# Average pooling on one Trainium2 core: the first tile loaded by four transfers of strided partitions

## The chip, the cores and the metric

The kernel runs on one core of a Trainium2 chip. The metric is the time of one execution on the device, in microseconds; the kernel before took 333.46 us, the median of three runs from 333.3 to 333.56. A core has engines that compute (here VectorE, called DVE in the profile, ScalarE or ACT, and GpSimd or POOL), a sequencer for issuing transfers (SyncE or SP), 16 DMA engines that move data between the device memory (HBM) and the on-chip memory (SBUF), and SBUF itself, which has 128 partitions. TensorE (PE) has no work in this kernel.

## The reference

The input `x` is 32 x 256 x 4096 in float32 and `output_size` is 256. Each output value is the mean of a window along the last axis:

```python
for i in range(output_size):
    start = int(i * length / output_size)
    end = int((i + 1) * length / output_size)
    result[:, :, i] = np.mean(x[:, :, start:end], axis=-1)
```

Since 4096 is 16 times 256, every window has 16 neighbouring values. The input is 134.22 MB and the output 8.39 MB, so the work is nearly all reading.

## The kernel before

Batch and channel are flattened into 8192 rows of 4096 values. A tile holds four of these rows in each of the 128 partitions, which is 64 KB per partition and 8 MB in all, and there are 16 tiles. For the first 15 tiles a partition owns 60 consecutive rows of HBM (`x_many`), and tile `t` takes the columns `t * cols` to `(t + 1) * cols` of them; the last tile has its own block of rows (`x_last`). So for each partition a tile is one contiguous run of 64 KB in HBM and one contiguous run in SBUF.

The tiles pass through a pool of two buffers (`inpool`, L53). The loop from L62 does for each tile:

- L70: SP issues one transfer of the whole tile, 128 partitions, into the buffer `xin`. All 16 loads go through SP's queue, in order.
- L72, in the last tile only: SP issues the store of the results of the first 15 tiles (`o_many`, 60 KB per partition).
- L73: POOL adds, for the upper half of the windows, the second eight values of each window to the first eight.
- L78: DVE sums the 16 values of each window of the lower half.
- L81: DVE sums the eight values that POOL left of each window of the upper half.
- L84: ACT multiplies the tile's 1024 results by 1/16.

After the loop two stores bring out the last tile's results, 4 KB per partition: partitions 0 to 119, then 120 to 127 (L89 and L90, which calls `store`, L57). At the very end SP waits until all three stores have landed (L95).

The order of work around L70 is set by the tile framework, which derives the waits from the program: a compute instruction that reads `xin` waits for the landing of what was loaded into it, and a load into a buffer waits until the instructions that read its former contents are done and until its former load has landed. With two buffers the loads of tiles 0 and 1 are issued at once, and the load of tile 2 waits for the compute of tile 0. On each DMA engine packets run in the order in which they were queued. A packet of a load is one partition's 64 KB.

Of the kernel before, what the change touches and what calls it, by code (L numbers as in the profile page):

```python
# [1 line left out]

# [4 lines left out]


@with_exitstack
def kernel(  # L10
    ctx: ExitStack,
    tc: tile.TileContext,
    x: bass.AP,
    output_size: int,
    out: bass.AP,
):

    nc = tc.nc
    F32 = mybir.dt.float32
    X = mybir.AxisListType.X

    batch, channels, length = x.shape
    ob, oc, olen = out.shape
    assert ob == batch and oc == channels and olen == output_size
    assert length % output_size == 0
    window = length // output_size  # L30
    hw = window // 2
    inv_w = 1.0 / float(window)

    P = nc.NUM_PARTITIONS
    R = 4
    rows = batch * channels
    assert rows % (P * R) == 0
    ntiles = rows // (P * R)
    many = (ntiles - 1) * R
    cells = R * output_size  # L40
    m = cells // 2
    cols = R * length

    xr = x.rearrange("b c l -> (b c) l")
    orow = out.rearrange("b c o -> (b c) o")
    x_many = xr[0 : P * many, :].rearrange("(p r) l -> p (r l)", p=P, r=many)
    o_many = orow[0 : P * many, :].rearrange("(p r) o -> p (r o)", p=P, r=many)
    x_last = xr[P * many :, :].rearrange("(p r) l -> p (r l)", p=P, r=R)
    o_last = orow[P * many :, :].rearrange("(p r) o -> p (r o)", p=P, r=R)

    res_many = nc.alloc_sbuf_tensor("res_many", [P, (ntiles - 1) * cells], F32, align_bytes=256)
    res_last = nc.alloc_sbuf_tensor("res_last", [P, cells], F32, align_bytes=256)
    inpool = ctx.enter_context(tc.tile_pool(name="inpool", bufs=2))  # L53

    stored = nc.alloc_semaphore("stored")

    def store(out, in_):  # L57
        ins = nc.sync.dma_start(out=out, in_=in_)
        tc.no_tile_sem_insts.add(ins.ins.name)
        ins.then_inc(stored, 16)  # L60

    for t in range(ntiles):  # L62
        last = t == ntiles - 1
        xin = inpool.tile([P, cells, window], F32, name="xin")
        if last:
            res, base, src = res_last, 0, x_last
        else:
            res, base = res_many, t * cells
            src = x_many[:, t * cols : (t + 1) * cols]
        nc.sync.dma_start(out=xin.rearrange("p o w -> p (o w)"), in_=src)  # L70
        if last:
            store(o_many, res_many[:, :])  # L72
        nc.gpsimd.tensor_add(  # L73
            out=xin[:, m:cells, 0:hw],
            in0=xin[:, m:cells, 0:hw],
            in1=xin[:, m:cells, hw:window],
        )
        nc.vector.reduce_sum(  # L78
            out=res[:, base : base + m], in_=xin[:, 0:m, :], axis=X
        )  # L80
        nc.vector.reduce_sum(  # L81
            out=res[:, base + m : base + cells], in_=xin[:, m:cells, 0:hw], axis=X
        )
        nc.scalar.mul(  # L84
            out=res[:, base : base + cells],
            in_=res[:, base : base + cells],
            mul=inv_w,
        )
    for lo, hi in ((0, 120), (120, P)):  # L89
        store(o_last[lo:hi, :], res_last[lo:hi, :])  # L90

    ctx.pop_all().close()
    tc.close()
    tc.compile()  # L94
    nc.sync.wait_ge(stored, 48)  # L95
    nc.sync.sem_clear(stored)


# [1 line left out]
_INS = ['x', 'output_size']  # L100
_OUTS = [((32, 256, 256), 'float32')]

_NUMBERS = {'output_size': 256}


# [26 lines left out]
```

## Time and profile before

| What | Value |
|---|---|
| Median of three runs | 333.46 us |
| The profiled execution's own time | 333.37 us |
| Its span | 332.1 us |
| DVE busy | 209.7 us, 32 instructions |
| POOL busy | 139.7 us, 20 instructions |
| ACT busy | 18.2 us, 17 instructions |
| DMA packets | 2599, 142.61 MB, 99.4% of 16 engines' span |
| First packets of tile 0 / tile 0 landed | 1.8 us / 22.7 us |
| One POOL add (L73) | 8.719 us |
| One DVE sum of 16 (L78) / of 8 (L81) | 8.686 us / 4.420 us |

The span runs from the first to the last instruction of the profile; the execution's own time is a little longer. Engine shares are busy time over the span. The DMA share is the time that packets took, over 16 engines, and a window's share counts each packet at its start, so in short windows it can lie over 100%. A line number such as L70 is a line of the kernel before. "SPq" is SP's sequencer, which issues transfers.

### The profile page before, as it was taken

The page shows a single profiled execution, that of the slowest core. Times are in us where ns is not written, and L with a number is a line of the kernel's source. Part 1 is how long each engine was busy: PE and PEld are TensorE (multiplying, and loading weights), DVE is VectorE, ACT ScalarE, POOL GpSimd, SP SyncE. Part 2 cuts the span into 40 slices and gives each one's busy share as a digit, 9 for nine tenths or more (in the row PEclk, how much of TensorE's full clock was granted, in tenths as well). Part 3 has the DMA queues.
Part 4 walks back from the last instruction along what each step waited for, and adds up shares of the span by engine and source line. Part 5 has one row for each costly group of instructions (what it writes and reads, how often), then busy time and mean ns, then how long its engine had stood idle before and what let it go on. Part 6 is the DMA issues. An engine that isn't in the chain of part 4 may idle for free.

```text
span 332.1 us, 160 instructions
## 1 busy us (share of the span) xinstructions
DVE 209.7 (63%) x32; ACT 18.2 (5%) x17; POOL 139.7 (42%) x20
## 2 busy tenths in 40 slices
DVE  0029396692939669293966939295693929569392
ACT  1000101001010100101010010101000010100001
POOL 0027091542709164270916427090643709063270
DMA  9898999989899998989899998989999898989997
GB/s 379 379 505 379 474 411 426 458 379 505 379 489 395 450 434 379 505 379 505 379 474 411 395 489 379 505 379 489 395 450 434 379 505 379 505 379 474 395 466 307
DMA packets 2599, 142.61 MB, mean 429 GB/s; under 512 B 295, under 2 KB 295, under 8 KB 423
## 3 DMA queue, kind: packets, MB, share of 16 engines
q1 hardware_dynamic: 2599, 142.61, 99.4%
HBM read 134.22 MB, written 8.39 MB: 429 GB/s over the span
## 4 chain that ended last, share of the span: by engine, by line
DMA 66%; POOL 18%; DVE 11%; POOLq 3%; issue 0%; ACT 0%; SPq 0%
DMA xin<-in_x_dram 66%; POOL xin L73 18%; DVE res_many L81 9%; POOLq L94 3%; DVE res_last L81 1%; ACT res_last L84 0%; SPq L70 0%; POOLq L73 0%
## 5 line engine op out<-in xcount | busy, mean ns | idle before, releaser
L73 POOL TENSOR_TENSOR xin<-xin 128x4096 f32<-128x4096 f32 x16 | 139.5, 8719 | 181.7 <-DMA xin<-in_x_dram 181.7
L78 DVE TENSOR_REDUCE res_many<-xin 128x512 f32<-128x8192 f32 x15 | 130.3, 8686 | 107.4 <-DMA xin<-in_x_dram 107.4
L81 DVE TENSOR_REDUCE res_many<-xin 128x512 f32<-128x4096 f32 x15 | 66.3, 4420 | 2.5 <-POOL xin L73 2.3
L84 ACT ACTIVATE res_many<-res_many 128x1024 f32<-128x1024 f32 x15 | 15.9, 1057 | 289.8 <-DVE res_many L81 289.8
L78 DVE TENSOR_REDUCE res_last<-xin 128x512 f32<-128x8192 f32 x1 | 8.7, 8686 | 6.3 <-DMA xin<-in_x_dram 6.3
L81 DVE TENSOR_REDUCE res_last<-xin 128x512 f32<-128x4096 f32 x1 | 4.4, 4420 | 0.2 <-POOL xin L73 0.2
L84 ACT ACTIVATE res_last<-res_last 128x1024 f32<-128x1024 f32 x1 | 1.1, 1057 | 18.5 <-DVE res_last L81 18.5
L84 ACT ACT_TABLE_LOAD x1 | 1.3, 1283 | 0.7 <-PEq L113 0.7
L113 POOL MEMSET const-float32-0.0<- 128x1 f32 x1 | 0.1, 99 | 0.2 <-issue 0.2
L113 POOL MEMSET const-bfloat16-1.0<- 128x1 bf16 x1 | 0.1, 103 | 0.0
L113 POOL MEMSET const-uint8-127<- 128x1 uint8 x1 | 0.1, 103 | 0.0
L113 POOL MEMSET const-float32-1.0<- 128x1 f32 x1 | 0.1, 99 | 0.0
## 6 DMA issues: line engine op xcount, KB each, us to landing
out_dram<-res_many SPq DMA_DIRECT2D x1, 7680.0 KB
out_dram<-res_last SPq DMA_DIRECT2D x1, 480.0 KB
xin<-in_x_dram SPq DMA_DIRECT2D x16, 25.3
out_dram<-res_last SPq DMA_DIRECT2D x1, 32.0 KB
```

Source lines behind the costliest of these rows:

```text
L73: nc.gpsimd.tensor_add(out=xin[:, m:cells, 0:hw], in0=xin[:, m:cells, 0:hw], in1=xin[:, m:cells, hw:window],)
L78: nc.vector.reduce_sum(out=res[:, base : base + m], in_=xin[:, 0:m, :], axis=X)
L81: nc.vector.reduce_sum(out=res[:, base + m : base + cells], in_=xin[:, m:cells, 0:hw], axis=X)
L84: nc.scalar.mul(out=res[:, base : base + cells], in_=res[:, base : base + cells], mul=inv_w,)
L94: tc.compile()
L113: nc = _bacc.Bacc("TRN2", target_bir_lowering=False, num_devices=1)
```

## The change

The load of tile 0 is cut into four transfers by partitions: 0, 8, .., 120 (16 partitions), then 4, 12, .., 124 (16), then 2, 6, .., 126 (32), then the odd ones (64). Together they cover the 128 partitions once. SP issues them one after the other in place of the single one. For every other tile the list `parts` holds the one entry (0, 1), which is all the partitions in one transfer as before. What is computed, the buffers, the stores and the rest of the order of the program stay as they are.

```diff
@@ -67,7 +67,10 @@
         else:
             res, base = res_many, t * cells
             src = x_many[:, t * cols : (t + 1) * cols]
-        nc.sync.dma_start(out=xin.rearrange("p o w -> p (o w)"), in_=src)
+        flat = xin.rearrange("p o w -> p (o w)")
+        parts = ((0, 8), (4, 8), (2, 4), (1, 2)) if t == 0 else ((0, 1),)
+        for lo, step in parts:
+            nc.sync.dma_start(out=flat[lo:P:step, :], in_=src[lo:P:step, :])
         if last:
             store(o_many, res_many[:, :])
         nc.gpsimd.tensor_add(
```

## The prediction

> **What bounds the kernel now.** I read the page first: engine shares, DMA rows, the chain that ended last.
>
> ```profile
> DVE 209.7 (63%) x32; ACT 18.2 (5%) x17; POOL 139.7 (42%) x20
> ...
> DMA packets 2599, 142.61 MB, mean 429 GB/s; under 512 B 295, under 2 KB 295, under 8 KB 423
> ...
> q1 hardware_dynamic: 2599, 142.61, 99.4%
> ...
> DMA xin<-in_x_dram 66%; POOL xin L73 18%; DVE res_many L81 9%; POOLq L94 3%; DVE res_last L81 1%; ACT res_last L84 0%; SPq L70 0%; POOLq L73 0%
> ```
>
> The 16 DMA engines are busy 99.4% of the span and no compute engine over 63%, so the end is set by the longest of 16 rows of packets laid end to end. The POOL and DVE shares of the chain are only where the chain jumps from one transfer to the compute that frees its buffer: work beside the packets, as the timeline of tiles 0 and 1 shows next.
>
> ```profile
> 22.72 8.69 DVE L78 TENSOR_REDUCE res_many<-xin 128x512 f32<-128x8192 f32 x1 [22.72 <-DMA xin<-in_x_dram]
> 22.76 8.72 POOL L73 TENSOR_TENSOR xin<-xin 128x4096 f32<-128x4096 f32 x1 [22.32 <-DMA xin<-in_x_dram]
> 31.51 4.42 DVE L81 TENSOR_REDUCE res_many<-xin 128x512 f32<-128x4096 f32 x1
> 35.96 19.61 SPq L70 DMA_DIRECT2D xin<-in_x_dram  x2
> ...
> 42.00 8.69 DVE L78 TENSOR_REDUCE res_many<-xin 128x512 f32<-128x8192 f32 x1 [6.07 <-DMA xin<-in_x_dram]
> ```
>
> Tile 0 lands at 22.7 us, its buffer is free and tile 2 asked for at 35.96, and tile 1 is still streaming until 42.0: 6.0 us of cover. So whatever delays tile 0's packets delays the end one for one, and whatever delays only waits or issues by less than 6 us does not.
>
> Last I asked the DMA view for single waves of packets. The share is of 16 engines over the window, so share x window is the mean packet where the window holds the starts of 16 packets. Windows, in order: 1.7 to 4.7 us, 4.7 to 7.1, 309 to 311.5, and 330.6 to 331.2.
>
> ```profile
> DMA packets 16, 1.05 MB, mean 350 GB/s; under 512 B 0, under 2 KB 0, under 8 KB 0
> ...
> q1 hardware_dynamic: 16, 1.05, 104.3%
> ```
> ```profile
> DMA packets 16, 1.05 MB, mean 437 GB/s; under 512 B 0, under 2 KB 0, under 8 KB 0
> ...
> q1 hardware_dynamic: 16, 1.05, 100.8%
> ```
> ```profile
> DMA packets 16, 1.05 MB, mean 419 GB/s; under 512 B 0, under 2 KB 0, under 8 KB 0
> ...
> q1 hardware_dynamic: 16, 1.05, 107.6%
> ```
> ```profile
> DMA packets 58, 0.24 MB, mean 396 GB/s; under 512 B 0, under 2 KB 0, under 8 KB 58
> ...
> q1 hardware_dynamic: 58, 0.24, 96.1%
> ```
>
> A load packet is one 64 KB row of a partition. In the first wave it takes 1.043 x 3.0 = 3.13 us, in the second 1.008 x 2.4 = 2.42 us (27.1 GB/s), which is the rate of the whole run: tiles land 19.3 us apart, eight packets of 2.42. The third window is the last wave of the last tile, when the large store has been issued and its reads of SBUF begin: 1.076 x 2.5 = 2.69 us. The fourth is the final store's 4 KB rows: 0.961 x 0.6 x 16 / 58 = 0.159 us each (25.8 GB/s).
>
> **The change, part by part.** The sum is made against the profiled execution, 333.37 us (span 332.1 and 1.27 around it), 0.09 under the median 333.46 of the runs.
>
> *Issues on SP.* Tile 0 takes four issues instead of one. An issue costs 0.41 us plus 0.06 of gap (0.74 to 1.21), so they go out at 0.74, 1.21, 1.68 and 2.15, and tile 1's at 2.62 instead of 1.21. From issue to first packet took 1.04 us (0.74 to 1.78, where the DMA view's first packets start). The second transfer's rows are therefore queued at 2.25, the third's at 2.72, the fourth's at 3.19, tile 1's at 3.66, while the engines need them at 4.8, 7.2, 12 and 22 at the earliest. Cost 0, hidden by the packets in flight; uncovered, each would cost 0.47.
>
> *Start.* The first transfer now has one row per engine. Its issue may shorten from 0.41 us towards the 0.29 of the 8-row store, and the two late starters (14 of 16 first packets start between 1.78 and 2.1, one near 2.25, one near 2.79) may come with the others. Bounds: no gain, and all of the first wave's excess, 3.13 - 2.42 = 0.71. Nearest row is the issue: I take -0.1.
>
> *Completions.* Each transfer ends with a 4-byte entry on every engine it uses. The final 2.1 us hold 39 of them, 16 + 15 + 8, which shows 16, 15 and 8 engines at work on 128, 120 and 8 rows; so 16, 16, 32 and 64 rows give every engine 1, 1, 2 and 4, eight in all as before. Three more entries at 9 ns (that window's 20.70 us of packets less 128 x 0.159, over 39) are +0.03.
>
> *Waits.* The first POOL and DVE instructions wait for four landings instead of one, and SP's wait before tile 2 (17 ns, at 22.7) becomes four; what is queued behind it, tile 2's issue, waits for DVE L81 until 35.96 anyway. Hidden by 13.2 us there and by the 6.0 us of tile 1's packets; 0. Beyond 6.0 us a delay would leave the engines empty.
>
> *Two engines at neighbouring rows.* This decides. A transfer of 128 rows takes every group of four neighbouring partitions, and so do those at strides 4 and 2. The two at stride 8 take every second group, with all 16 engines at once. The trace of before has no strided load, so bounds: nothing, if an engine's 2.42 us is its own limit; and twice the time, if it is the limit of one of 16 paths into SBUF, each serving its own groups of neighbouring partitions: half the groups then hold half the paths, and two engines use one. Two packets per engine would take 4.84 us instead of 2.42, together +4.84. Rows towards nothing: the 4 KB rows of the final store, where 15 engines read 120 rows, eight each, and then eight engines read eight neighbouring rows, at 0.159 us throughout. Towards a cost: the 2.69 us wave, the one place where a load's writes meet a second stream on the SBUF side, at +0.27 a packet (two packets: +0.54); and that load rows from HBM and the large store's 60 KB rows to HBM (1.030 x 2.2 = 2.27 us in the window from 314 to 316.2) run at the same 27.1 GB/s, so that the ceiling is not HBM's direction. The changed operation is a write of 64 KB rows, nearer to the load rows, which sit exactly on that ceiling in every wave, than to short reads. I take the full price, less what a pair wins by not starting together (starts differ by 0.1 to 0.3 us): +4.6. A gain is excluded, since the 2.42 us wave is already the fastest in the trace.
>
> [...]
>
> [...]
>
> Sum: 333.37 + 0 - 0.1 + 0.03 + 0 + 4.6 = 337.9.
>
> **The rivals.**
> *No sharing, no change.* The engines' rate is their own and tile 0's rows only come in another order. Then 333.37 - 0.1 + 0.03 = 333.3, between 332.8 and 334.0. The store's rows speak for it, the load's constant rate against it.
>
> *Faster.* The one-row transfer removes most of the first wave's excess and its late start, on the engines that end last. It decides from 0.67 us (0.2%) on; the ceiling is 0.71 mean, so 332.7. Against: 3.13 us is seen on nearly all engines, the late one included, and an engine with one row queued still has to wait for its first bytes.
>
> *A wait between the four transfers.* If each is issued only when the one before has landed, an engine runs dry at three joins, at about 1.04 from issue to packet and 0.71 of a first packet: 3 x 1.75 = 5.3, 338.6. If the queues only restart, 3 x 0.71 = 2.1, 335.5. Against: the four write different partitions, and tiles 0 and 1 went out 0.47 apart without a gap.
>
> **How the numbers follow.** A repeat run differs by 0.1 us; 0.2%, 0.67 us, is about what a measurement tells from no change. Sharing 0.50 (own range 337.2 to 338.6; a milder sharing down to 334.5 is another 0.05); wait or restart 0.05; no change 0.31; faster 0.09. Slower holds 0.50 + 0.05 + 0.05 = 0.60, within 0.2% 0.31, faster 0.09. The two large cases lie on both ends, so the range must span 333 to 338.6: I give 332.9 to 338.7, which leaves out most of the faster case and the worst waits, about 0.12.
>
> **What would show it.** Right: tile 0 lands at about 27.3 us instead of 22.7, with two waves of packets near 4.8 us each before 12 us and waves of 2.42 after; every later landing shifted by the same 4.6; 2647 packets, 343 of them under 512 B; 19 load issues. Wrong: first two waves at 3.1 and 2.4 (no sharing); slices of idle DMA in the first 10 us (a wait); a landing before 22.2 (faster). It would also be wrong if the late start moved to an engine that carries nine rows of the final store, which I hold under 0.3 us.

## The result and the profile after

The changed kernel takes 338.36 us, the median of four runs (338.02 to 338.40), against 333.51 us (333.30 to 333.69) for the kernel before: a ratio of 1.0144, with a 95% interval from 1.0132 to 1.0156. The profiled execution took 338.35 us with a span of 337.0, 4.98 more than that of before (333.37, span 332.1). Line numbers of the changed kernel are three higher from the load on: L73 is the load, L76 POOL's add, L81 and L84 DVE's sums.

The page of the changed kernel shows the same compute and the same bytes, with 48 more packets, all of them 4-byte completion entries (three more transfers on 16 engines):

```profile
DVE 209.7 (62%) x32; ACT 18.2 (5%) x17; POOL 139.7 (41%) x20
...
GB/s 249 249 498 373 498 373 498 373 498 373 498 373 498 373 490 381 490 381 474 397 459 412 420 451 420 451 412 459 389 482 381 490 381 490 373 498 373 482 467 296
DMA packets 2647, 142.61 MB, mean 423 GB/s; under 512 B 343, under 2 KB 343, under 8 KB 471
...
q1 hardware_dynamic: 2647, 142.61, 99.3%
```

The DMA engines are as busy as before, 99.3%, but in the first two of the 40 slices (16.9 us) they move 249 GB/s, where the kernel before moves 379, as its own row shows:

```profile
GB/s 379 379 505 379 474 411 426 458 379 505 379 489 395 450 434 379 505 379 505 379 474 411 395 489 379 505 379 489 395 450 434 379 505 379 505 379 474 395 466 307
```

Busy engines with less to show for it: the packets themselves got longer. The timeline says where the delay stops:

```profile
27.91 8.69 DVE L81 TENSOR_REDUCE res_many<-xin 128x512 f32<-128x8192 f32 x1 [27.91 <-DMA xin<-in_x_dram]
27.95 8.72 POOL L76 TENSOR_TENSOR xin<-xin 128x4096 f32<-128x4096 f32 x1 [27.51 <-DMA xin<-in_x_dram]
36.71 4.42 DVE L84 TENSOR_REDUCE res_many<-xin 128x512 f32<-128x4096 f32 x1
41.16 0.34 SPq L73 DMA_DIRECT2D xin<-in_x_dram  x1
...
47.11 8.69 DVE L81 TENSOR_REDUCE res_many<-xin 128x512 f32<-128x8192 f32 x1 [5.98 <-DMA xin<-in_x_dram]
```

Tile 0 lands at 27.9 us instead of 22.7, tile 1 at 47.1 instead of 42.0. The first shift is 5.2 us and the second 5.1: all of the loss is in tile 0, and the tiles behind it are moved whole (the end moves by only 4.9; the last wave of loads gives 0.27 back, as the point on the evidence below shows). Tile 2 is still asked for 6 us before the engines run out of tile 1 (41.16 against 47.11), so no wait was added.

The DMA view of the changed kernel, for its first four waves of packets. The windows are 2 to 5 us, 6.4 to 8.4, 11.3 to 13.3 and 14.7 to 16.7, and each holds the starts of 16 load packets:

```profile
q1 hardware_dynamic: 16, 1.05, 163.4%
...
q1 hardware_dynamic: 32, 1.05, 247.9%
...
q1 hardware_dynamic: 32, 1.05, 148.2%
...
q1 hardware_dynamic: 16, 1.05, 121.0%
```

Share times window is the mean packet: 1.634 x 3.0 = 4.90 us, 2.479 x 2.0 = 4.96, 1.482 x 2.0 = 2.96 and 1.210 x 2.0 = 2.42. The second and third also hold 16 completion entries of about 18 ns, so their load packets take 4.94 and 2.95. Before, the four waves took 3.13, 2.42, 2.42 and 2.42. The differences are 1.77, 2.52 and 0.53, together 4.82 us, which is two packets of 2.42 to within 0.02. They stand in three waves and not in two; a reading of that, not tried further, is that in the first wave the longer packets cover the 0.71 us that first packets lost anyway, and the third wave pays it back.

### The profile page after: what moved, and what is told of

Read it like the earlier page. It is cut to its first block, busy times and chain, and to the rows that moved or that the text cites. A ratio compares the mean times of both kernels' runs of the same rounds, so it can differ in the third digit from the quotient of the medians.

```text
span 337.0 us, 168 instructions
## 1 busy us (share of the span) xinstructions
DVE 209.7 (62%) x32; ACT 18.2 (5%) x17; POOL 139.7 (41%) x20
## 2 busy tenths in 40 slices
DMA packets 2647, 142.61 MB, mean 423 GB/s; under 512 B 343, under 2 KB 343, under 8 KB 471
## 3 DMA queue, kind: packets, MB, share of 16 engines
q1 hardware_dynamic: 2647, 142.61, 99.3%
## 4 chain that ended last, share of the span: by engine, by line
DMA 66%; POOL 18%; DVE 11%; POOLq 3%; SPq 1%; issue 0%; ACT 0%
DMA xin<-in_x_dram 66%; POOL xin L76 18%; DVE res_many L84 9%; POOLq L97 3%; DVE res_last L84 1%; SPq L73 1%; ACT res_last L87 0%; POOLq L76 0%
## 5 line engine op out<-in xcount | busy, mean ns | idle before, releaser
L76 POOL TENSOR_TENSOR xin<-xin 128x4096 f32<-128x4096 f32 x16 | 139.5, 8719 | 186.3 <-DMA xin<-in_x_dram 186.3
L81 DVE TENSOR_REDUCE res_many<-xin 128x512 f32<-128x8192 f32 x15 | 130.3, 8686 | 112.3 <-DMA xin<-in_x_dram 112.3
L84 DVE TENSOR_REDUCE res_many<-xin 128x512 f32<-128x4096 f32 x15 | 66.3, 4420 | 2.5 <-POOL xin L76 2.3
L81 DVE TENSOR_REDUCE res_last<-xin 128x512 f32<-128x8192 f32 x1 | 8.7, 8687 | 6.0 <-DMA xin<-in_x_dram 6.0
L84 DVE TENSOR_REDUCE res_last<-xin 128x512 f32<-128x4096 f32 x1 | 4.4, 4419 | 0.2 <-POOL xin L76 0.2
```

Of the source, the lines that this page charges most:

```text
L76: nc.gpsimd.tensor_add(out=xin[:, m:cells, 0:hw], in0=xin[:, m:cells, 0:hw], in1=xin[:, m:cells, hw:window],)
L81: nc.vector.reduce_sum(out=res[:, base : base + m], in_=xin[:, 0:m, :], axis=X)
L84: nc.vector.reduce_sum(out=res[:, base + m : base + cells], in_=xin[:, m:cells, 0:hw], axis=X)
```

## The experiments

Two theories stood beside the one predicted. The prediction's: when a transfer takes only every second group of four neighbouring partitions, two of the 16 DMA engines have to share one of the paths over which transfers reach SBUF. The paths are a supposition that no trace shows; what the runs can show is how long packets take with each arrangement of partitions. Rival 1: small transfers of strided rows are slow in themselves. Rival 2: the rows of HBM are what is slow, since the strided transfers also read HBM in longer strides.

### Strided transfers that take every group of four

```diff
-        parts = ((0, 8), (4, 8), (2, 4), (1, 2)) if t == 0 else ((0, 1),)
+        parts = ((0, 4), (2, 4), (1, 2)) if t == 0 else ((0, 1),)
```

> Tile 0 in three strided transfers, partitions 0, 4, .. (32), 2, 6, .. (32) and the odd ones (64), so that each takes every group of four neighbouring partitions. Theory (two engines share one path into SBUF when only every second group is taken): the slow waves vanish, packets 2.42 us from the second wave on, 333.5 to 334.0 (up to 0.4 for a later start). Rival 1 (several small transfers are slow in themselves, whatever the rows): each of the two small ones costs about 2.4, 336 to 338. Rival 2 (strided rows in HBM are slow): the stride in HBM stays large, 336 to 338.

It took 333.88 us, against 333.46 for the kernel before on the same chip, a ratio of 1.0010 (1.0001 to 1.0019). The DMA view of its first two waves, 2 to 5 us and 5.1 to 7.5:

```profile
q1 hardware_dynamic: 16, 1.05, 105.2%
...
q1 hardware_dynamic: 16, 1.05, 100.8%
```

These are 3.16 and 2.42 us, the packets of the kernel before. The transfers are still strided, small (32, 32 and 64 rows) and several, and the slow waves are gone. Rival 1 falls for transfers of 32 rows; those of 16 come up again below. What is left, 0.42 us, is partly a later start: the chain of this run has a first issue of 0.54 us where before it was 0.41, and the first packets start at 2.06 instead of 1.78, which is 0.28.

### The same partitions, other rows of HBM

```diff
+        row = 0
         for lo, step in parts:
-            nc.sync.dma_start(out=flat[lo:P:step, :], in_=src[lo:P:step, :])
+            n = (P - lo + step - 1) // step
+            nc.sync.dma_start(out=flat[lo:P:step, :], in_=src[row : row + n, :])
+            row += n
```

> The four transfers write the same strided partitions as the change, but read consecutive rows of HBM (0 to 15, 16 to 31, 32 to 63, 64 to 127), so tile 0's rows land in other partitions and its outputs are permuted. Theory (sharing on the SBUF side): nothing changes, first two waves near 4.9 us, 338.2 to 338.5. Rival 2 (strided rows in HBM are slow): the waves fall back to 3.1 and 2.4, 333.5 to 334.0.

338.62 us, a ratio of 1.0153 (1.0140 to 1.0167). Its first two waves, 2 to 5 us and 6.6 to 8.6 in the DMA view:

```profile
q1 hardware_dynamic: 16, 1.05, 164.8%
...
q1 hardware_dynamic: 32, 1.05, 244.4%
```

4.94 and 4.89 us (4.87 without the completion entries). HBM is now read in consecutive rows of `src`, and the loss is the same to within 0.3 us (5.16 against 4.85; the time is 0.1 above the 338.2 to 338.5 expected). So rival 2 falls too: the cost belongs to the partitions that are written.

### Nothing strided, but half of the partitions

```diff
-        parts = ((0, 8), (4, 8), (2, 4), (1, 2)) if t == 0 else ((0, 1),)
-        for lo, step in parts:
-            nc.sync.dma_start(out=flat[lo:P:step, :], in_=src[lo:P:step, :])
+        parts = ((0, 64), (64, P)) if t == 0 else ((0, P),)
+        for lo, hi in parts:
+            nc.sync.dma_start(out=flat[lo:hi, :], in_=src[lo:hi, :])
```

> Tile 0 in two transfers of 64 consecutive partitions, 0 to 63 and 64 to 127; nothing is strided and each transfer is 4 MB. [...] Rivals 1 and 2 (small transfers, strided HBM rows): neither is there, 333.5 to 334.0.

354.44 us, a ratio of 1.0629 (1.0614 to 1.0643): 21.0 us more, from two plain transfers of 4 MB, where both rivals have 333.5 to 334.0. If half of the partitions hold half of the paths, as the prediction supposed, all eight packets of an engine take 4.84 us, which is an estimate of 8 x 2.42 = 19.4 us more, 352.8; the time is 1.6 above that. The third wave of this run (11.8 to 14 us in the DMA view):

```profile
q1 hardware_dynamic: 16, 1.05, 233.2%
```

2.332 x 2.2 = 5.13 us a packet, 2.12 times 2.42. So neither the stride nor the small size is needed; 64 neighbouring partitions are enough for packets of a little more than twice the length (5.13 against 4.84). That two engines share a path is still only the reading that fits; which of the partitions would lie on one was not mapped here beyond these arrangements.

### Four engines on a path

The last run's kernel with other cuts of tile 0:

```diff
-        parts = ((0, 64), (64, P)) if t == 0 else ((0, P),)
+        parts = [(k, k + 16) for k in range(0, P, 16)] if t == 0 else ((0, P),)
```

> Tile 0 in eight transfers of 16 consecutive partitions. Theory (engines share a path by groups of neighbouring partitions): 16 consecutive partitions are four groups, four engines on each path, packets of 9.7 to 10.3 us, tile 0 in eight such waves, +58 to +63, 392 to 397. If two engines on a path were a fixed penalty rather than a share: packets near 4.9 as in the change, +20, 353 to 355.

387.29 us, a ratio of 1.1615 (1.1594 to 1.1637), in a window of the DMA view that holds the fourth wave, 28.1 to 31 us:

```profile
q1 hardware_dynamic: 32, 1.05, 318.7%
```

3.187 x 2.9 = 9.24 us a packet with its completion entry, 3.8 times 2.42. The length grows with the number of engines that the theory puts on a path (2.42 us for one, 4.94 in the change and 5.13 with halves for two, 9.24 for four), so it is a share and not a fixed penalty. The time is 5 us below the lower end of what was expected, mostly because each of an engine's eight packets takes 9.2 us and not 9.7. These transfers have 16 rows, as the two strided ones of the change have, and their packets take 9.2 us and not 4.94: with the same size, the partitions decide, and no loss is left for rival 1 to explain.

### Reads of SBUF, in the large store

The kernel before, with the store of the first 15 tiles' results cut in two (the wait at the end counts 64 instead of 48, for the fourth store):

```diff
         if last:
-            store(o_many, res_many[:, :])
+            for lo, hi in ((0, 64), (64, P)):
+                store(o_many[lo:hi, :], res_many[lo:hi, :])
```

> Loads as in the kernel before; the large store of the first 15 tiles' results (60 KB rows) is cut into partitions 0 to 63 and 64 to 127, with all else as it was. If reads of SBUF share paths as writes do: eight packets of 2.27 us become 4.53 each, +18.1, 351 to 352. If reads don't, as the final store's 4 KB rows at 0.159 us suggest: 333.3 to 334.0.

352.38 us, a ratio of 1.0568 (1.0552 to 1.0584), just above the 351 to 352 that sharing would give. The prediction had held the full-rate 4 KB rows of the final store against the sharing; this run shows that stores lose by such a cut as loads do. The DMA view of its first and of a later store wave makes the contradiction visible (311.8 to 314 us, then 323.2 to 325):

```profile
q1 hardware_dynamic: 32, 0.98, 103.8%
...
q1 hardware_dynamic: 16, 0.98, 268.5%
```

The first wave of 60 KB packets takes 1.038 x 2.2 = 2.28 us, full rate, and a later one 2.685 x 1.8 = 4.83. The first packets of a store look as if they shared nothing. That suggested that an engine reads ahead: it begins the reads of the first packet while the packet before it is still being written.

The next run tries the final store's own arrangement on the large store's rows (again with 64 for 48 in the last wait):

```diff
-            for lo, hi in ((0, 64), (64, P)):
+            for lo, hi in ((0, 120), (120, P)):
```

> Loads as before; the large store with its 60 KB rows is cut as the final store is, partitions 0 to 119 and 120 to 127, so that the arrangement whose 4 KB rows ran at full rate is tried with long rows. If that arrangement is free for reads: only one more 2.27 us packet on eight engines, 335 to 336. If the short rows were at full rate because they had been read ahead (32 KB per engine is less than one packet of the store before): packets near 4.5 to 4.8 us for the 120 rows after the first wave, longer still for the eight, 355 to 363.

359.80 us, a ratio of 1.0791 (1.0771 to 1.0811). From 337.9 to 342.9 us in its DMA view:

```profile
q1 hardware_dynamic: 17, 1.04, 100.4%
```

1.004 x 5.0 x 16 / 17 = 4.72 us a packet, where the uncut store takes 2.27. The arrangement that looked free with 4 KB rows costs twice the time with long ones. Both runs change what a store reads of SBUF together with the order of the rows it writes in HBM; that the reads are what is shared is carried over from the loads, as no run varies the HBM rows of a store alone.

The direct test takes the cover away: let the final store's rows be the first on idle engines. A first attempt moved the call that issues the large store behind the loop of the final two:

```diff
-        if last:
-            store(o_many, res_many[:, :])
...
     for lo, hi in ((0, 120), (120, P)):
         store(o_last[lo:hi, :], res_last[lo:hi, :])
+    store(o_many, res_many[:, :])
```

> The large store is moved behind the two final stores, so that the final 4 KB rows (120 partitions, then eight) start on DMA engines that have been idle since about 312 us, with no earlier packets under which their reads could be hidden. If the 4 KB rows were at full rate in the kernel before only because they were read ahead: mean near 0.3 us for the rows of the 120 (two engines on a path), more for the eight. If reads of this arrangement and size share nothing: 0.159 us again. Either way the large store's 18.1 us now stand behind the end of the compute: 346 to 349 in time.

It took 333.54 us against 333.62, a ratio of 1.0000 (0.9989 to 1.0011), and its timeline has the large store where it was, issued at 307.95 us (307.67 before): the place of the call in the program didn't decide when the store was issued, so this run says nothing about reads and is only another look at the kernel before. The second attempt issues the large store after the framework has closed:

```diff
-        if last:
-            store(o_many, res_many[:, :])
...
     tc.compile()
+    nc.sync.dma_start(out=o_many, in_=res_many[:, :]).then_inc(stored, 16)
     nc.sync.wait_ge(stored, 48)
```

> The large store is issued after the tile framework's last barrier, so that SP really issues it behind the two final stores; their 4 KB rows then start on DMA engines that have been idle since about 312 us. If the 4 KB rows were at full rate in the kernel before only because they were read ahead under earlier packets: mean near 0.3 us for the rows of the 120 (two engines on a path), more for the eight. If reads of this arrangement and size share nothing: 0.159 us again. Either way the large store's 18.1 us now stand behind the end of the compute: 346 to 350 in time.

350.21 us, a ratio of 1.0504 (1.0473 to 1.0534), just above the range. The DMA view of the final rows, 327.9 to 328.5 us, 327.9 to 328.9, and 329.2 to 329.8:

```profile
q1 hardware_dynamic: 36, 0.15, 109.7%
...
q1 hardware_dynamic: 49, 0.20, 96.1%
...
q1 hardware_dynamic: 51, 0.20, 84.6%
```

The first 36 rows take 1.097 x 0.6 x 16 / 36 = 0.293 us, near twice the 0.159 of the kernel before. The same rows take longer without earlier packets to hide under, as sharing would have it. A slow start of idle engines could also make rows longer (the first load packets took 3.13 us and the next 2.42), but then each engine's first row should be the longer one, and here the first rows are the shorter ones: the 11 that start from 327.9 to 328.07 us take 0.229 us on the mean (92.7% of 0.17 us), the 13 from 328.5 to 328.9 take 0.37 (15.38 us of packets in the second window less 10.53 in the first). So sharing is the reading that fits; no run here puts 4 KB rows of all 128 partitions on idle engines, which would test it. The later ones (0.846 x 0.6 x 16 / 51 = 0.159) are at full rate again; whether the engines had then fallen out of step or had read ahead among themselves, these runs don't tell.

### Where the late start comes from

The three transfers of the first experiment, for tile 1 instead of tile 0:

```diff
-        parts = ((0, 4), (2, 4), (1, 2)) if t == 0 else ((0, 1),)
+        parts = ((0, 4), (2, 4), (1, 2)) if t == 1 else ((0, 1),)
```

> The three strided transfers that take every group of four (0, 4, ..; 2, 6, ..; the odd ones) for tile 1 instead of tile 0; tile 0 in one transfer. If the 0.4 us that they cost on tile 0 is the later start (first issue 0.54 instead of 0.41 us, first packets 2.06 instead of 1.78): first packets at 1.78 again and 333.3 to 333.6. If three transfers cost 0.4 us wherever they stand: 333.9.

333.60 us against 333.36, a ratio of 1.0004 (0.9995 to 1.0014). The start of its chain of waits beside that of the changed kernel, first this run's, with start and length in us:

```profile
0.73 0.41 SPq L73
1.14 0.06 issue
1.21 0.53 SPq L73
1.73 0.05 issue
1.78 0.61 SPq L73
```
```profile
0.73 0.61 SPq L73
1.34 0.06 issue
1.40 0.57 SPq L73
1.97 0.05 issue
2.02 0.58 SPq L73
```

The first issue is back to 0.41 us and the first packets start at 1.77, as expected. The time lies on the border between the two answers, 333.3 to 333.6 and 333.9, and its interval takes in no difference at all: inconclusive on the last 0.2 us. A longer first issue and later first packets go together in these traces: 0.41 us with 1.78 and 1.77, 0.54 with 2.06, 0.61 with 2.12. But the issue is only a part of the delay: from its end to the first packet it takes 0.63 us in the kernel before (1.15 to 1.78) and 0.78 in the changed kernel (1.34 to 2.12), so of the 0.34 us 0.20 lies in the issue and 0.14 behind it. Why both are longer is not shown. It isn't the number of rows alone, since the run with sixteens has a first issue of 0.38 us for 16 consecutive partitions, against 0.61 for 16 strided ones. Nor is it the stride alone, since the 64 consecutive partitions of the run with halves have one of 0.55:

```profile
0.73 0.55 SPq L73
```

## Why the prediction held, point by point

**The range.** It ran from 332.9 to 338.7 and so took in both no change and full sharing; that 338.36 lies inside says little, and 0.50 was all that sharing had been given. What the traces bear out is the deciding term and, with it, the sum of 337.9.

**What bounds the kernel.** Right. A delay of tile 0's packets reached the end almost one for one, 5.2 us at tile 0's landing and 4.9 in the span. The waits are hidden as it said: tile 2 is asked for 5.95 us before tile 1 lands.

**Issues on SP.** Right that they are hidden, wrong in size: 0.57 to 0.61 us each instead of 0.41. The second transfer's rows came well before the engines asked at 6.4 us: its issue ended at 1.97. That packets run in the order of their transfers shows in the kernel before, where the last 64 KB packet starts at 309.8 us, the 60 KB ones from 311.9 to 328.3, and the first 4 KB one at 330.0.

**Start.** Wrong in sign. The term was -0.1, from the row of the 8-row store (0.29 us); the first issue took 0.61 instead of 0.41, and the first packets start 0.34 us later (2.12 against 1.78), not earlier. This is the step that failed: a short transfer's row was taken for that of a strided one, and nothing was allowed for the time behind the issue. The late starter didn't come with the others either (14 of 16 first packets start between 2.12 and 2.5, the last at 2.93).

**Completions.** Three more entries were put at 9 ns. In the slow waves they take about 18; with the entries of tile 0 the sum stays under 0.1 us.

**Two engines at neighbouring rows.** Right in what it foresaw of the packets: 4.94 us where every second group is taken, 2.42 where every group is, and by the same theory 5.13 with halves and 9.24 with sixteens. The 16 paths into SBUF behind it were the author's supposition; no run shows paths or their number. The size was 4.84 less 0.24 for pairs that don't start together; the waves show 4.82, so the deduction was wrong: getting ahead within a pair won nothing that the waves show. What the prediction set out as signs came true with it: tile 0 at 27.9 us (27.3 forecast), two waves near 4.9 before 12 us, 2647 packets, 343 of them under 512 B, 19 load issues. Only the third wave, 2.95 instead of 2.42, was not foreseen.

**The evidence against it.** The final store's 4 KB rows, which the prediction set towards nothing, were a row whose cover had not been seen: they run behind earlier packets, and take nearly double when that cover goes (0.293 us against 0.159). The other row, the 2.69 us wave of the last tile, was no measure of the change's cost either: in the changed kernel the same wave takes 2.42, in the DMA view from 313.9 to 316.4 us:

```profile
q1 hardware_dynamic: 16, 1.05, 96.7%
```

That gives back 0.27 us. The traces show a pattern. The wave takes 2.42 in all four runs whose tile 0 has slow waves (the change, the other rows of HBM, the halves, the sixteens), and 2.60 to 2.78 in all six that have none and let the large store follow at once. In the run that issues the large store at the end it takes 2.42 (96.7% of 2.5 us from 309 us on), so the long wave goes with the store behind it, as the prediction read it. Why slow waves of the first tile take it away is open.

**The sum.** Taken against the profiled execution: late start 0.34, packets 4.82, less 0.27 at the last load wave: 4.89, against 4.98 in the profiled execution and 4.85 between the medians. The prediction had 4.53, with 0.44 missing at the start and 0.22 in the deduction, and 0.27 too much for want of the last wave. It came within 0.5 us of the measured time partly because these cancel.

**The rivals.** No sharing would have left 2.42 us in the second wave, and it was 4.94. A wait between the transfers would have left the engines idle between the first two waves, but on the mean the second starts where the first ends (2.29 + 4.90 = 7.19 us). Faster had the first wave's excess for it, and that didn't go: with cuts that share nothing, in the first experiment, the first wave still takes 3.16 us. The prediction's reading that the late starter shows the 3.13 too was off: the packet that starts at 2.79 us takes 2.64.

## What to carry to other kernels

When a kernel's end is set by DMA engines that are always busy, look at the length of single packets before and after an edit, not at the busy share: both kernels here show 99%. Where a transfer is cut, it matters which partitions each piece takes: all 128, or pieces at strides of two and four, kept 2.42 us for a row of 64 KB here, from the second wave on; pieces of 64 neighbouring partitions, or of every eighth, took 5.13 and 4.94, and pieces of 16 neighbouring ones 9.2. A row at full rate behind other packets doesn't prove that nothing is shared: the 4 KB rows of the final store took 0.159 us there and 0.293 as the first on idle engines.

## What the runs showed of the hardware that was not expected

- A DMA engine seems to read ahead across transfers: the first 60 KB packets of the cut store, behind the last loads, took 2.28 us and later ones 4.83, and 4 KB rows went from 0.159 to 0.293 us without cover. That it does is the reading that fits both; no trace here shows an engine's reads by themselves.
- Against the even split of the theory, 4.84 us for two engines and 9.68 for four, packets were slightly longer with 64 neighbouring partitions (5.13 us, 2.12 times 2.42) and in the changed kernel (4.94, 2.04 times), and slightly shorter with 16 neighbouring ones (9.2 us, 3.8 times). If four engines do share one path, it carries, by an estimate from that packet, 4 x 64 KB in 9.2 us, 28.5 GB/s, a little more than the 27.1 that an engine moves in the 2.42 us waves.
- The first issue took a different time with different partitions: 0.41 us for 128, 0.38 for 16 consecutive ones and 0.55 for 64, 0.54 for 32 and 0.61 for 16 strided ones, each as the first in its program.
- No version tried here beats the kernel before; the nearest that cuts tile 0 is the one with strides 4, 4 and 2, at 0.1% slower.
